# A hybrid decoder layer on one core: where group 0's down projection stands in the first feed-forward, and in which order VectorE takes the mixer's modulation sums

## The chip, the core and the metric

The kernel runs on one core of a Trainium2 chip. The metric is the device time of one execution in microseconds; the time given for a kernel is the median of its runs. The engines are TensorE (PE, with its weight loads PEld), VectorE (DVE), ScalarE (ACT), GpSimd (POOL) and SyncE (SP), whose queue issues all of the transfers spoken of here. In the profile every instruction recorded through the small wrapper class of this kernel has the line L107, so instructions are told apart by their tiles.

## What is computed

One layer of a decoder over 1024 tokens of width 1024, in float32, with a feed-forward (hidden width 2816) ahead of a mixer and another behind it:

```python
(sh1, sc1, g1, sh2, sc2, g2, sh3, sc3, g3) = jnp.split(c_act @ w_mod[l] + b_mod[l], N_MOD, axis=-1)

h = modulate(rms_norm(x, ffn1_norm[l]), sh1, sc1)
x = x + 0.5 * g1[:, None, :] * swiglu(h, ffn1_w_gate[l], ffn1_w_up[l], ffn1_w_down[l])

h = modulate(rms_norm(x, mix_norm[l]), sh2, sc2)
b_gate, c_gate, v, u = jnp.split(h @ w_in[l], [D_CONV, 2 * D_CONV, 3 * D_CONV], axis=-1)
y_conv = short_conv_mixer(b_gate, c_gate, v, conv_w[l])
y_ssm = s5_mixer(u, ...)
y_mix = jnp.concatenate([rms_norm(y_conv, ...), rms_norm(y_ssm, ...)], axis=-1)
x = x + g2[:, None, :] * (y_mix @ w_out[l])

h = modulate(rms_norm(x, ffn2_norm[l]), sh3, sc3)
x = x + 0.5 * g3[:, None, :] * swiglu(h, ffn2_w_gate[l], ffn2_w_up[l], ffn2_w_down[l])
return rms_norm(x, final_norm)
```

`swiglu(h, wg, wu, wd)` is `(silu(h @ wg) * (h @ wu)) @ wd`.

## The kernel before

**Products.** Each float32 operand is split into a high and a low part, and a product takes three matmuls (`mm3`: high by high, high by low, low by high) of 128 x 128 by 128 x 512. The tokens are two halves of 512 (`h` = 0, 1). The hidden width is 11 groups (`NGRP`) of 256, the model width 8 blocks of 128 (`d` or `k`). A group's first part is its gate and up projection, its second part its down projection.

**The first feed-forward.** Groups 0 to 3 are projected plainly, groups 4 to 10 by `seven`, a scheme of Strassen's kind with seven products in place of eight; their activations ("lefts") go to DRAM tiles `kept[g]` (`keep`, an SP transfer for each). The second part of groups 1 to 4 and of 5 to 8 follows, by seven products again, in two calls of `down7` ("fad0", "fad1"). Each call makes two passes p = 0, 1 over seven products; a product takes four lefts of 512 KB each and one granule of weights. Passes p = 0 and 1 write the blocks d = 0, 1, 4, 5 and 2, 3, 6, 7. The lefts of chunk 0 are fetched during group 10's up side, those of chunk 1 during p = 1 of fad0 (`fetch_chunk`, through the argument `then`). Groups 0, 9 and 10 (`LAST[0]`) remain: `last_parts` does them together, for four blocks d and one token half at a time (d outside, h inside), 2 x 2 x 3 x 8 calls of `mm3`, and adds the sum to x by one `scalar_tensor_tensor` for each (d, h). Their activations are fetched by `fetch_last` in p = 1 of fad1, at the products A11, A12 and A22. `after1` squares and sums the new x for the mixer's norm; with the last block of a half it starts that half's norm, whose results `h2` (16 tiles) the mixer's first projection `u` reads. `u` takes four weight tiles at once.

**Weights.** `Weights` holds the weights' order: `stream` lists the raw arrays (1 MB each; two raw buffers) and granules (pairs of pieces). `pump` takes a free slot (three in `ringp`, a fourth in `ring1b` for the mixer), copies the high part on ACT and computes the low part on VectorE; sums of pieces for the seven-product schemes are made on POOL. A raw buffer is loaded again when all of its pieces are split. In the first feed-forward the last arrays are `wl1`, three raw arrays for groups 0, 9 and 10.

**x.** x is not held during the projections. `open_x` gives it space when group 10 starts; `load_x` fetches its eight 512 KB tiles, four then and four at the product A12 of p = 0 of fad0.

**Space.** The pool "A" of `mov` has 20 tiles of 512 KB, the pool "B" (`movB1`) 12. They hold the modulated input and its combinations, the lefts, the tiles that `keep` stores, the modulation weights of the first side work, and `h2`.

**Side work.** A `Clock` counts calls of `mm3`; every `period` ticks it steps a generator. `side2` does modulation sums: `mod_fetch` loads a 512 KB tile `wm` over SP, `mod_tile` multiplies and sums it on VectorE (1.14 to 1.23 us), 24 sums for three vectors, with two tiles in flight. It runs once from fad1 on (period 8) for the vectors of the mixer, and once in the mixer for those of the second feed-forward: added with period 8 ahead of the last `gate_b` calls, stopped by period 1000 ahead of `glu`, and stepped again with period 3 from `w_out((2, 3), 1, 0)` on; a loop behind `w_out((4, 5, 6, 7), 0, 1)` steps what is left, ahead of the norm `n3` of the second feed-forward's input `h3`.

**Order.** The compiler's scheduler orders each engine's instructions by its own simulated times: an instruction whose operands are there in the simulation goes ahead of an earlier one that still waits. Only where `InOrder.strict` is set (the prologue) does the wrapper tie each instruction to the one before it on its engine. An engine runs its queue in the order so fixed.

Of the kernel before, what the change touches and what calls it, by code (L numbers as in the profile page):

```python
# [17 lines left out]
ALU = mybir.AluOpType  # L18
# [3 lines left out]
P = 128  # L22
# [6 lines left out]
NGRP = NF // 2  # L29
# [6 lines left out]

CHUNKS = 2

LAST = ((0, NGRP - 2, NGRP - 1), (NGRP - 2, NGRP - 1))
J = S // TAU  # L40
NB = 8
GB = G // NB
# [16 lines left out]
class Clock:  # L59
# [2 lines left out]

    def __init__(self, period):
        self.now, self.period, self.n, self.since = 0, period, 0, 0
        self.due, self.side = [], deque()

    def after(self, ticks, fn):
        self.n += 1
# [10 lines left out]

    def step(self):  # L80
        if self.side:
            try:
                next(self.side[0])
            except StopIteration:
                self.side.popleft()

    def until(self, done):
        while not done():
# [8 lines left out]
class InOrder:  # L97


    strict = False  # L100

    def __init__(self, tc, engine):
        self.tc, self.engine, self.last = tc, engine, None

    def __getattr__(self, name):
        def call(*args, **kw):
            r = getattr(self.engine, name)(*args, **kw)  # L107
            if self.last is not None and InOrder.strict:
                info = mybir.DependencyInfo(mybir.DependencyClass.NoSync, mybir.DependencyReason.DATA)
                self.tc.add_manual_dep(r.ins, self.last.ins.name, info, reason="order of issue")  # L110
            self.last = r
            return r

        return call
# [114 lines left out]


@with_exitstack
def hymba_layer(ctx: ExitStack, tc, x_d, wm1_d, wmod_d, gu1_d, gs1_d, ds1_d, wl1_d, win_d, wout_d, glu_d, gu2_d, gs2_d, wd2_d, ds2_d, wl2_d, cols_d, cond_d, lam_d, bc_d, out_d):
    nc = tc.nc
    V, A, T, SP = (InOrder(tc, e) for e in (nc.vector, nc.scalar, nc.tensor, nc.sync))

# [51 lines left out]
    def stream(gu, gs, wd, ds, wl, m):  # L287


        for g in range(m):  # L290
            plain([gu[2 * g], gu[2 * g + 1]])
        for g in range(m, NGRP):
            j = len(srcs)
            inner = g == 1
            srcs.extend([gs[g - m, 0], wd, gs[g - m, 1]] if inner else [gs[g - m, 0], gs[g - m, 1]])
            seven = [(i, c) for i in (j, j + 1 + inner) for c in Weights.SEVEN]
            seven = [seven[i : i + 2] for i in range(0, 14, 2)]
            if inner:
                granules.extend(seven[:1] + [[(j + 1, 2 * q), (j + 1, 2 * q + 1)] for q in range(2)] + seven[1:])
            else:  # L300
                granules.extend(seven)
        for c in range(CHUNKS):
            for p in range(2):
                j = len(srcs)
                srcs.extend([ds[c, p, 0], ds[c, p, 1]])
                granules.extend([(j, s), (j + 1, s)] for s in Weights.SECOND)
        plain([wl[i] for i in range(wl.shape[0])])

    stream(gu1_d, gs1_d, None, ds1_d, wl1_d, SEVEN_FROM[0])
    plain([win_d[i] for i in range(8)] + [glu_d] + [wout_d[i] for i in range(4)])  # L310
    stream(gu2_d, gs2_d, wd2_d, ds2_d, wl2_d, SEVEN_FROM[1])
    ws = Weights((V, A, SP, nc.gpsimd), srcs, granules, 2)
# [517 lines left out]
    def kept_for(g, all_seven=True):  # L830

        names = [left for left, _ in SEVEN] if all_seven else ["A11", "A12", "A21", "A22"]
        return {left: scratch.tile([P, 2, HALF], F32, name=f"kept{g}{left}") for left in names}

    kept = {g: kept_for(g, g not in LAST[0]) for g in range(NGRP)}
    afs = {}
    for fi in range(2):
        for i in (2 * fi, 2 * fi + 1):
# [331 lines left out]
                gu_keep(fi, h, pg[h], proj(wu, act[h], f"{name}u{fi}_{h}"), afs, kept, name)  # L1170
            ws.free()

    movs["B"] = es1.enter_context(tc.tile_pool(name="movB1", bufs=12))
    sums_open, first_open = sums_opened()
    clock.side.append(side1())
    clock.period = 4
# [1 line left out]
        gate_up(act1, f"fa{g}", kept[g], g == SEVEN_FROM[0] - 1)  # L1178
    clock.period = 7.75
    lefts = [{left: [] for left, _ in SEVEN} for _ in range(CHUNKS)]  # L1180
    a_last = [{} for _ in LAST[0]]
    HOMES = dict(A11="A", S2="B", A12="A", S3="B", S1="B", A22="A", S4="A")

    def fetch_chunk(c, left, name="fa"):
        for g in range(1 + 4 * c, 5 + 4 * c):
            lefts[c][left].append(fetch(kept[g], left, HOMES[left], f"{name}{g}l"))

    def fetch_last(left):

        if left in ("A11", "A12", "A22"):  # L1190
            i = ("A11", "A12", "A22").index(left)
            for h in range(2):
                for fi in range(2):
                    a_last[i][fi, h] = fetch(kept[LAST[0][i]], f"A{h + 1}{fi + 1}", "A", f"fa{LAST[0][i]}l")

    for g in range(SEVEN_FROM[0], NGRP):
        if g == NGRP - 1:
            while clock.side:
                clock.step()
            side_open.close()  # L1200
            first_open.close()
            open_x(ctx)
            load_x(range(2), (0, 2))
        if g == NGRP - 2:
            pools.pop("first")
        seven(f"fa{g}", lambda: None, kept=kept[g], then=(lambda left: fetch_chunk(0, left)) if g == NGRP - 1 else None)
    down7("fad0", lefts[0], 0, lambda left: fetch_chunk(1, left), lambda left: load_x(range(2), (1, 3)) if left == "A12" else None)
    clock.period = 8
    clock.side.append(side2(mod_mov, (SC2, SH2, G2)))
    down7("fad1", lefts[1], 0, fetch_last)  # L1210
    ws.sums_pool = None
    sums_open.close()
    ring1_open = ExitStack()

    def last_parts():
        for dh in range(2):
            wd = ws.take(3)
            for h in range(2):
                outs = [ps(f"fald{4 * dh + i}_{h}") for i in range(4)]
                for q, (w, a) in enumerate(zip(wd, a_last)):  # L1220
                    for fi in range(2):
                        for i, o in enumerate(outs):
                            mm3(o[:], w, 4 * fi + i, a[fi, h], q == fi == 0, q == 2 and fi == 1)
                    if h:
                        ws.free()
                for i, o in enumerate(outs):
                    d = 4 * dh + i
                    V.scalar_tensor_tensor(out=x[d][h], in0=o[:], scalar=gate[:, 0, d : d + 1], in1=x[d][h], op0=ALU.mult, op1=ALU.add)
                    after1(d, h)

    last_parts()
    while clock.side:
        clock.step()
    es1.close()
    ring1 = ring1_open.enter_context(tc.tile_pool(name="ring1b", bufs=1, side="right"))
    ws.open(ring1, 1)
    ws.pump()


    es2 = ExitStack()  # L1240
# [170 lines left out]
    pools["cact"] = wmp.tile([P, 1024], F32, name="cact2")  # L1411
    SP.dma_start(pools["cact"][:], cact_d[:])
    clock.period = 8
    clock.side.append(side2(lambda name: wmp.tile([P, 1024], F32, tag="wm", name=name, bufs=2)[:], (SC3, SH3, G3)))
    for i in range(4):
        across(i, lambda d, t: SP.dma_start(t, d), y_d, yb[i])
# [66 lines left out]
    while clock.side:  # L1483
        clock.step()
    clock.period = 4
    mods_open.close()
    es2.close()
    movs["B"] = ctx.enter_context(tc.tile_pool(name="movB", bufs=12))
# [35 lines left out]

    clock.side.extend([combos(act3, "h3", "BAA"), combos_last(act3, "h3", "A")])
    a_prev = group0()
    kept = {g: kept_for(g, g not in LAST[1]) for g in range(1, NGRP - 1)}
    HOMES = dict(A11="B", S2="A", A12="B", S3="A", S1="B", A22="A", S4="A")
    lefts = [{left: [] for left in HOMES} for _ in range(CHUNKS)]
    a_last = {}  # L1530
# [67 lines left out]
def _arrays(i):  # L1598
# [5 lines left out]
    for n in (1, 2):  # L1604
        g, u = _tiles(i[f"ffn{n}_w_gate"][0]), _tiles(i[f"ffn{n}_w_up"][0])
        wd = i[f"ffn{n}_w_down"][0]
        m = SEVEN_FROM[n - 1]

        b = wd.reshape(NGRP, 2, P, 2, 512)
        if n == 2:  # L1610
            a["wd2"] = b[0].transpose(1, 2, 0, 3).reshape(P, 2, 1024)
        b = b[list(LAST[n - 1])].transpose(3, 0, 2, 1, 4).reshape(-1, 2, P, 1024)
        a[f"wl{n}"] = b.transpose(0, 2, 1, 3)

        b = wd.reshape(NGRP, 2, P, 2, 2, 2, P)[1 : 1 + 4 * CHUNKS].reshape(CHUNKS, 2, 2, 2, P, 2, 2, 2, P)
# [24 lines left out]
    return {k: np.ascontiguousarray(v) for k, v in a.items()}  # L1640


_ORDER = ["x", "wm1", "wmod", "gu1", "gs1", "ds1", "wl1", "win", "wout", "glu", "gu2", "gs2", "wd2", "ds2", "wl2", "cols", "cond", "lam", "bc"]


# [15 lines left out]
```

## Time and profile before

| | us |
|---|---|
| median of 3 runs | 1750.19 |
| lowest, highest | 1748.85, 1751.76 |
| the profiled execution | 1752.1 |
| its span, first to last instruction | 1750.3 |
| PE busy in the span | 1677.9 |
| DVE busy | 1300.6 |
| ACT busy | 566.0 |
| POOL busy | 351.1 |

The mean granted clock of TensorE is 0.989 of full. The profile has a page with busy times, groups and the chain of waits, and views of single stretches: a table of stretches (busy time of each engine with the number of instructions, the granted clock, the share of time in which the 16 DMA engines were busy, GB/s), the instructions of one engine in order of time (start, length, engine, line, operation, output and inputs, count, and in brackets the idle time before and what ended it), the waits in total, and the transfers with their time from issue to landing. The stretches of the first feed-forward in the profile are group 10's first part from 467 to 505, fad0 from 505 to 590, fad1 from 590 to 668, and the last parts from 668 to 736.

### The profile page before, as it was taken

Reading aid. Unit: us, or ns where it says so; the run is one execution under the profiler, and the core shown is the slowest. Engines: PE = TensorE matmul, PEld = TensorE weight load, DVE = VectorE, ACT = ScalarE, POOL = GpSimd, SP = SyncE. Lnnn points to the kernel's source line nnn. Section 1 sums busy time; section 2 is a strip of 40 time slices with the busy share of each in tenths; the row PEclk is TensorE's granted clock in tenths of the full one; section 3 lists DMA queues with packets and bytes.
Section 4 is the critical chain, followed back from the end, with each engine's and each line's share of the span. In section 5 each row is a group of like instructions: output and inputs, shape, how many; then the busy total and the mean of one; then the engine's idle time right before and its main releaser. Section 6 shows DMA issues by size and latency. Waiting matters only on the chain.

```text
span 1750.3 us, 20808 instructions
## 1 busy us (share of the span) xinstructions
PE 1677.9 (96%) x7532; PEld 1379.6 (79%) x7532; DVE 1300.6 (74%) x2286; ACT 566.0 (32%) x934; POOL 351.1 (20%) x241
## 2 busy tenths in 40 slices
PE   4999999999999999999999899989999999999996
PEld 3788887878787888887877778778888888888886
DVE  7999999999855687744656977967777666676656
ACT  4223234444322221332113424423343443322221
POOL 0000132222222221100000022023323322333211
PEclk9999999999999999999999999999999999999998
DMA  8245544444597877134654450113444334669312
GB/s 319 85 145 196 207 167 165 182 169 178 196 391 266 326 256 292 56 84 149 210 157 140 144 191 25 48 46 135 157 162 173 147 133 156 239 242 366 115 49 96
DMA packets 101080, 304.54 MB, mean 174 GB/s; under 512 B 19057, under 2 KB 34673, under 8 KB 89842
## 3 DMA queue, kind: packets, MB, share of 16 engines
q1 hardware_dynamic: 100978, 303.22, 48.4%
q8 instruction: 59, 0.97, 0.2%
q14 instruction: 43, 0.35, 0.1%
HBM read 212.47 MB, written 86.51 MB: 171 GB/s over the span
## 4 chain that ended last, share of the span: by engine, by line
PE 76%; DVE 14%; DMA 5%; issue 2%; POOL 1%; ACT 1%; SPq 1%; DVEq 0%; POOLq 0%; ACTq 0%
PE wo L107 4%; PE fald L107 3%; DVE w L107 3%; PE p L107 2%; PE fb10d L107 2%; PE fbd_0B L107 2%; PE fbd_1B L107 2%; PE u L107 2%; DMA swz<-si 2%; PE b L107 1%; DVE x L107 1%; PE c L107 1%; PE fa3u L107 1%; PE fb0g L107 1%; PE fa2g L107 1%
## 5 line engine op out<-in xcount | busy, mean ns | idle before, releaser
L107 ACT CAST w<-raw 128x512 fp32r<-128x512 f32 (+1 forms) x358 | 236.2, 689 | 484.3 <-issue 75.0
L107 DVE TENSOR_TENSOR w<-raw,w 128x512 fp32r<-128x512 f32 (+1 forms) x358 | 295.9, 845 | 107.3 <-ACT w L107 106.5
L164 POOL TENSOR_TENSOR sums<-raw 128x512 f32<-128x512 f32 x50 | 71.4, 1429 | 451.5 <-DMA raw<-in_gs 263.3
L173 POOL TENSOR_TENSOR raw<-sums,raw 128x512 f32<-128x512 f32 x50 | 77.7, 1554 | 371.1 <-DVE w L107 358.9
L175 POOL TENSOR_TENSOR raw<-raw 128x512 f32<-128x512 f32 x50 | 77.5, 1549 | 89.6 <-DVE w L107 73.0
L107 DVE CUSTOM_DVE_ANT_0 wm<-wm,cact 128x1024 f32<-128x1024 f32 x56 | 76.6, 1375 | 16.9 <-DMA wm<-in_wmod 16.9
L165 POOL TENSOR_TENSOR raw<-raw 128x512 f32<-128x512 f32 x50 | 77.3, 1547 | 3.2
L366 POOL TENSOR_TENSOR n3aq<-n3aq,n3aq 128x512 f32<-128x512 f32 x5 | 8.3, 1666 | 281.4 <-DMA wm<-in_wmod 255.7
L107 PE MATMUL p<-h,w 128*128 128x512 f32 x192 | 50.0, 423 | 8.0 <-DVE h L107 5.1
L107 DVE TENSOR_TENSOR w<-sums,w 128x512 fp32r<-128x512 f32 x50 | 52.5, 1063 | 3.6 <-ACT w L107 3.0
L107 PEld LDWEIGHTS p<-h,w 128*128 128x128 f32 x192 | 39.4, 207 | 18.4 <-DVE h L107 6.4
L107 PE MATMUL v<-h,w 128*128 128x512 f32 x192 | 46.9, 395 | 0.0
L107 PE MATMUL c<-h,w 128*128 128x512 f32 x192 | 46.6, 395 | 0.0
L107 PE MATMUL wo<-oa,w 128*128 128x512 f32 x192 | 45.6, 392 | 0.9 <-DVE w L107 0.7
L107 PE MATMUL b<-h,w 128*128 128x512 f32 x192 | 45.6, 394 | 0.0
L107 PE MATMUL wo<-ob,w 128*128 128x512 f32 x192 | 45.5, 392 | 0.0
L107 PE MATMUL u<-h,w 128*128 128x512 f32 x192 | 44.7, 392 | 0.2 <-DVE h L107 0.2
L107 PEld LDWEIGHTS wo<-oa,w 128*128 128x128 f32 x192 | 35.8, 188 | 9.0 <-DVE w L107 1.1
L107 PEld LDWEIGHTS u<-h,w 128*128 128x128 f32 x192 | 35.7, 188 | 8.2 <-DVE h L107 0.6
L107 PEld LDWEIGHTS wo<-ob,w 128*128 128x128 f32 x192 | 35.8, 188 | 7.7 <-DVE ob L107 0.4
L107 PEld LDWEIGHTS b<-h,w 128*128 128x128 f32 x192 | 35.6, 188 | 7.1
L107 PEld LDWEIGHTS c<-h,w 128*128 128x128 f32 x192 | 35.4, 188 | 7.0
(1565 smaller groups left out, 4056.2 us busy)
## 6 DMA issues: line engine op xcount, KB each, us to landing
raw<-in_gs SPq DMA_DIRECT2D x34, 1024.0 KB, 5.5
wm<-in_wmod SPq DMA_DIRECT2D x56, 512.0 KB, 5.3
raw<-in_ds SPq DMA_DIRECT2D x16, 1024.0 KB, 7.2
raw<-in_gu SPq DMA_DIRECT2D x10, 1024.0 KB, 7.0
mw<-in_wm SPq DMA_DIRECT2D x8, 1024.0 KB, 12.8
x<-in_x SPq DMA_DIRECT2D x16, 512.0 KB, 8.0
raw<-in_win SPq DMA_DIRECT2D x8, 1024.0 KB, 5.4
raw<-in_wl SPq DMA_DIRECT2D x5, 1024.0 KB, 6.7
```

What stands on the lines that cost most here:

```text
L107: r = getattr(self.engine, name)(*args, **kw)
L164: self.G.tensor_tensor(out=f, in0=r[2], in1=r[1], op=ALU.subtract)
L165: self.G.tensor_tensor(out=r[1], in0=r[1], in1=r[0], op=ALU.subtract)
L173: self.G.tensor_tensor(out=r, in0=s["t3"], in1=r, op=ALU.add)
L175: self.G.tensor_tensor(out=r, in0=self.chunk(j, 3), in1=r, op=ALU.subtract)
L366: nc.gpsimd.tensor_tensor(out=a, in0=a, in1=sq[:, :n], op=ALU.add)
```

## The change

Four things are changed. Group 0's second part is done by itself, by `down2`, directly behind group 10's first part and ahead of fad0; its weights are a raw array of their own (`wd1`) behind group 10's, its activations are fetched where chunk 0's A11 lefts were, and these are fetched behind `down2` in the program. x is loaded whole when group 10 starts. The last parts are groups 9 and 10 alone, by `down`, with the token half outside and the blocks inside; the pool `movB1` is closed and the fourth slot `ring1b` opened ahead of them, and the four weight tiles are taken at once and given back at the end; the period there is 7. And in the mixer's side work each VectorE instruction of a step is tied to the VectorE instruction issued before it in the program (`pinned`).

```diff
-LAST = ((0, NGRP - 2, NGRP - 1), (NGRP - 2, NGRP - 1))
+LAST = (NGRP - 2, NGRP - 1)
...
     def step(self):
         if self.side:
+            if self.pin is not None:
+                self.pin.pinned = True
             try:
                 next(self.side[0])
             except StopIteration:
                 self.side.popleft()
+            if self.pin is not None:
+                self.pin.pinned = False
...
-            if self.last is not None and InOrder.strict:
+            if self.last is not None and (InOrder.strict or self.pinned):
...
+        if m > 1:
+            plain([wd])
...
-    stream(gu1_d, gs1_d, None, ds1_d, wl1_d, SEVEN_FROM[0])
+    stream(gu1_d, gs1_d, wd1_d, ds1_d, wl1_d, SEVEN_FROM[0])
...
-    movs["B"] = es1.enter_context(tc.tile_pool(name="movB1", bufs=12))
+    movB1_open = ExitStack()
+    movs["B"] = movB1_open.enter_context(tc.tile_pool(name="movB1", bufs=12))
...
+    def fetch_all(tiles, g):
+        for h in range(2):
+            for fi in range(2):
+                tiles[fi, h] = fetch(kept[g], f"A{h + 1}{fi + 1}", "A", f"fa{g}l")
+
+    def fetch_now(left):
+
+        if left == "A11":
+            fetch_all(a_first, 0)
+        else:
+            fetch_chunk(0, left)
+
     def fetch_last(left):
 
-        if left in ("A11", "A12", "A22"):
...
+        if left in ("A11", "A12"):
+            i = ("A11", "A12").index(left)
+            fetch_all(a_last[i], LAST[i])
...
-            load_x(range(2), (0, 2))
+            load_x(range(2))
...
-        seven(f"fa{g}", lambda: None, kept=kept[g], then=(lambda left: fetch_chunk(0, left)) if g == NGRP - 1 else None)
-    down7("fad0", lefts[0], 0, lambda left: fetch_chunk(1, left), lambda left: load_x(range(2), (1, 3)) if left == "A12" else None)
-    clock.period = 8
+        seven(f"fa{g}", lambda: None, kept=kept[g], then=fetch_now if g == NGRP - 1 else None)
+    down2(a_first, 0, "fa0", (0, 1))
+    fetch_chunk(0, "A11")
+    down7("fad0", lefts[0], 0, lambda left: fetch_chunk(1, left))
+    clock.period = 7
     clock.side.append(side2(mod_mov, (SC2, SH2, G2)))
     down7("fad1", lefts[1], 0, fetch_last)
     ws.sums_pool = None
     sums_open.close()
+    movB1_open.close()
     ring1_open = ExitStack()
-
-    def last_parts():
...
-    last_parts()
+    ring1 = ring1_open.enter_context(tc.tile_pool(name="ring1b", bufs=1, side="right"))
+    ws.open(ring1, 1)
+    ws.pump()
+    w = ws.take(4)
+    for h in range(2):
+        down(h, [w[0], w[2], w[1], w[3]], a_last, 0, "fal", after1)
+    ws.free(4)
     while clock.side:
         clock.step()
     es1.close()
-    ring1 = ring1_open.enter_context(tc.tile_pool(name="ring1b", bufs=1, side="right"))
-    ws.open(ring1, 1)
-    ws.pump()
...
     clock.period = 8
+    clock.pin = V
     clock.side.append(side2(lambda name: wmp.tile([P, 1024], F32, tag="wm", name=name, bufs=2)[:], (SC3, SH3, G3)))
...
     clock.period = 4
+    clock.pin = None
...
-        if n == 2:
-            a["wd2"] = b[0].transpose(1, 2, 0, 3).reshape(P, 2, 1024)
-        b = b[list(LAST[n - 1])].transpose(3, 0, 2, 1, 4).reshape(-1, 2, P, 1024)
+        a[f"wd{n}"] = b[0].transpose(1, 2, 0, 3).reshape(P, 2, 1024)
+        b = b[list(LAST)].transpose(3, 0, 2, 1, 4).reshape(-1, 2, P, 1024)
```

`down2` is the helper that the second feed-forward already uses for its group 0: for four blocks d and a token half at a time it computes each output in a PSUM bank of its own (two calls of `mm3`) and adds it to x at once; a weight tile is given back after its four blocks.

More of the change, by code (lines that the diff above doesn't have):

```diff
@@ L64, in __init__ @@
         self.now, self.period, self.n, self.since = 0, period, 0, 0
-        self.due, self.side = [], deque()
+        self.due, self.side, self.pin = [], deque(), None
     def after(self, ticks, fn):
@@ L102, in __init__ @@
     def __init__(self, tc, engine):
-        self.tc, self.engine, self.last = tc, engine, None
+        self.tc, self.engine, self.last, self.pinned = tc, engine, None, False
     def __getattr__(self, name):
@@ L231, in hymba_layer @@
 @with_exitstack
-def hymba_layer(ctx: ExitStack, tc, x_d, wm1_d, wmod_d, gu1_d, gs1_d, ds1_d, wl1_d, win_d, wout_d, glu_d, gu2_d, gs2_d, wd2_d, ds2_d, wl2_d, cols_d, cond_d, lam_d, bc_d, out_d):
+def hymba_layer(ctx: ExitStack, tc, x_d, wm1_d, wmod_d, gu1_d, gs1_d, wd1_d, ds1_d, wl1_d, win_d, wout_d, glu_d, gu2_d, gs2_d, wd2_d, ds2_d, wl2_d, cols_d, cond_d, lam_d, bc_d, out_d):
     nc = tc.nc
@@ L293, in stream @@
             j = len(srcs)
-            inner = g == 1
+            inner = g == m == 1
             srcs.extend([gs[g - m, 0], wd, gs[g - m, 1]] if inner else [gs[g - m, 0], gs[g - m, 1]])
@@ L833, in kept_for @@
         return {left: scratch.tile([P, 2, HALF], F32, name=f"kept{g}{left}") for left in names}
-    kept = {g: kept_for(g, g not in LAST[0]) for g in range(NGRP)}
+    kept = {g: kept_for(g, 0 < g < NGRP - 2) for g in range(NGRP)}
     afs = {}
@@ L1180, in hymba_layer @@
     lefts = [{left: [] for left, _ in SEVEN} for _ in range(CHUNKS)]
-    a_last = [{} for _ in LAST[0]]
+    a_first, a_last = {}, [{} for _ in LAST]
     HOMES = dict(A11="A", S2="B", A12="A", S3="B", S1="B", A22="A", S4="A")
@@ L1186, in fetch_chunk @@
             lefts[c][left].append(fetch(kept[g], left, HOMES[left], f"{name}{g}l"))
-    def fetch_last(left):
-        if left in ("A11", "A12", "A22"):
[L1191 to L1194, printed above, removed]
+    def fetch_all(tiles, g):
[7 more added lines that the diff above has]
+            fetch_chunk(0, left)
+    def fetch_last(left):
+        if left in ("A11", "A12"):
+            i = ("A11", "A12").index(left)
+            fetch_all(a_last[i], LAST[i])
     for g in range(SEVEN_FROM[0], NGRP):
@@ L1212, in hymba_layer @@
     sums_open.close()
+    movB1_open.close()
     ring1_open = ExitStack()
-    def last_parts():
[L1216 to L1229, printed above, removed]
-    last_parts()
+    ring1 = ring1_open.enter_context(tc.tile_pool(name="ring1b", bufs=1, side="right"))
[5 more added lines that the diff above has]
+    ws.free(4)
     while clock.side:
@@ L1526, in hymba_layer @@
     a_prev = group0()
-    kept = {g: kept_for(g, g not in LAST[1]) for g in range(1, NGRP - 1)}
+    kept = {g: kept_for(g, g not in LAST) for g in range(1, NGRP - 1)}
     HOMES = dict(A11="B", S2="A", A12="B", S3="A", S1="B", A22="A", S4="A")
@@ L1640, in _arrays @@
     return {k: np.ascontiguousarray(v) for k, v in a.items()}
-_ORDER = ["x", "wm1", "wmod", "gu1", "gs1", "ds1", "wl1", "win", "wout", "glu", "gu2", "gs2", "wd2", "ds2", "wl2", "cols", "cond", "lam", "bc"]
+_ORDER = ["x", "wm1", "wmod", "gu1", "gs1", "wd1", "ds1", "wl1", "win", "wout", "glu", "gu2", "gs2", "wd2", "ds2", "wl2", "cols", "cond", "lam", "bc"]
 def kernel(**inputs):
```

## The prediction

> **What bounds the kernel now.** I read the page's head first, then a table of stretches, then the order of instructions on TensorE (PE) in the stretches that lose time.
>
> ```profile
> span 1750.3 us, 20808 instructions
> PE 1677.9 (96%) x7532; PEld 1379.6 (79%) x7532; DVE 1300.6 (74%) x2286; ACT 566.0 (32%) x934; POOL 351.1 (20%) x241
> ```
>
> PE is the bound, and no matmul is added or removed. So the change can only win or lose in the 72 us in which PE stands, and in the lower granted clock around such a stand. The table of stretches (start:end, length, busy PE, PEld, DVE, ACT, POOL, granted clock, DMA share, GB/s) shows where that is near the change:
>
> ```profile
> 505.00:527.00 22.00, 22.00 (x99) 18.24 (x98) 13.87 (x20) 6.16 (x11) 2.16 (x2) 1.00 1.00 368
> 543.40:562.60 19.20, 15.34 (x49) 11.13 (x49) 10.79 (x11) 5.09 (x10) 11.38 (x8) 0.82 0.51 190
> 724.00:755.00 31.00, 29.79 (x140) 23.84 (x141) 24.04 (x53) 10.51 (x16) 2.59 (x2) 1.00 0.19 69
> 975.00:986.00 11.00, 7.09 (x31) 5.84 (x32) 9.61 (x26) 4.01 (x6) 0.00 (x0) 0.90 0.42 138
> 1029.00:1036.00 7.00, 6.12 (x26) 4.45 (x25) 7.00 (x7) 3.03 (x4) 5.77 (x3) 1.00 0.49 142
> 1143.00:1156.00 13.00, 10.42 (x37) 7.54 (x36) 12.46 (x20) 1.24 (x2) 3.40 (x1) 0.87 0.00 1
> ```
>
> The largest loss that the first part of the change can reach is 543.4 to 562.6, in the first chunk's second projection (`down7` "fad0"), at the turn from p = 0 to p = 1. PE's own rows there, with the idle time and its releaser in brackets, and a row of the chain of waits for twelve undisturbed matmuls:
>
> ```profile
> 543.74 0.74 PE L107 MATMUL fad_0A<-fa1lA,w 128*128 128x512 f32 x2 [0.31 <-ACT w L107]
> 546.66 0.57 PE L107 MATMUL fad_0A<-fa1lA,w 128*128 128x512 f32 x1 [1.71 <-DVE w L107]
> 556.58 1.52 PE L107 MATMUL fad_0B<-fa3lS,w 128*128 128x512 f32 x3 [1.81 <-ACT w L107]
> 562.78 2.72 PE fad_0A L107 x12
> ```
>
> Two lefts with two outputs each are computed there, 4 x 12 matmuls: 4 x 2.72 = 10.9 us. They take 19.2, so 8.3 us are lost: 0.31 + 1.71 + 1.81 = 3.8 idle and 4.5 at the lower clock (0.82 in the table). The wait is for split weights, and behind them for the raw weights:
>
> ```profile
> 543.07 0.62 ACT L107 CAST w<-raw 128x512 fp32r<-128x512 f32 x1 [14.26 <-DMA raw<-in_ds]
> 527.80 1.30 DVE L107 TENSOR_TENSOR w<-raw,w 128x512 fp32r<-128x512 f32 x2 [0.48 <-ACT w L107]
> 529.73 0.32 SPq L107 DMA_DIRECT2D kept10A<-fa10A  x1
> 530.15 0.37 SPq L107 DMA_DIRECT2D fa1lS<-kept1S  x1
> 532.98 1.28 SPq L107 DMA_DIRECT2D raw<-in_ds  x2
> 480.00:500.00 20.00, 20.00 (x90) 16.55 (x89) 7.70 (x12) 6.30 (x12) 6.29 (x5) 1.00 1.02 407
> 500.00:520.00 20.00, 20.00 (x90) 16.59 (x89) 16.50 (x22) 7.42 (x13) 6.37 (x5) 1.00 1.00 376
> 520.00:540.00 20.00, 20.00 (x90) 16.59 (x89) 10.92 (x16) 2.81 (x5) 0.00 (x0) 1.00 0.87 322
> ```
>
> The buffers of p = 0 are free about 528, but the load goes out at 533, in SP's order behind group 10's last store (held to 529.7, until its tile was computed), four lefts and an x tile. It then lands at 543, ten us later, in a stretch whose DMA engines are full. What fills them is the fetching of a whole chunk of lefts (28 tiles of 512 KB) just as the first product begins.
>
> **The change part by part.** *Group 0 moved ahead.* Its 16 outputs x 2 x 3 = 96 matmuls go from the last parts to 505 to 527: 8 x 2.72 = 21.8 us of PE, moved, not added; net 0. The 16 outputs of groups 9 and 10 keep their 16 additions into x, so `down2` adds 16 on VectorE:
>
> ```profile
> L107 DVE SCALAR_TENSOR_TENSOR x<-fald,gate,x x16: 746/751/751, 683.2 to 744.8; 128x512 f32<-128x512 f32 x16
> PE fb0d L107 <- DVE x L107: 5.1, 4, 2.0
> ```
>
> That is 16 x 0.75 = 12.0 us. One output takes PE 6 matmuls, 1.36 us, so VectorE keeps pace, with six PSUM banks (8.2 us) between. It was busy 13.9 of 22 us in this stretch, of which the adds of fad0 (505 to 527) move on. The last parts lose four fetches and one of three raw loads to the stages ahead of fad0; nothing waits for these there now. I cost this at 0; where the cover is gone, the same helper in the second feed-forward gives the price: PE waited 5.1 us there, VectorE being full (12.46 of 13 us).
>
> What it brings is time: fad0 starts 21.8 us later, and the fetches of its lefts do not. At the turn to p = 1, now about 565, the first chunk's lefts and all of x have landed, the stores of group 10 are long out, and the raw load finds an emptier DMA. The later turns show what it then needs:
>
> ```profile
> raw<-in_ds SPq DMA_DIRECT2D x16, 1024.0 KB, 7.2
> 614.85 0.93 SPq L107 DMA_DIRECT2D raw<-in_ds  x2
> 631.13 0.50 PE L107 MATMUL fad_0A<-fa7lA,w 128*128 128x512 f32 x1 [1.14 <-DVE w L107]
> ```
>
> Five us from the queue and three from the landing (10 to 7.2) are more than the 3.8 us of idle. I take the whole 8.3 us back; the bounds are 0 and -8.3. The second chunk's turn (1.14 us idle, held by weights again) stays as it is: its modulation sums are stepped every 7 ticks instead of 8, 176 ticks / 7 = 25 steps against 208 / 8 = 26, as dense per stage; 0, bounds -1.1 and +1.1.
>
> A rule speaks for a smaller prize. The Trainium skill, TensorE: Matmul & The Clock Gate, Part 1 (The HAM clock gate), has the clock fall only after an idle window of about 3.4 us. No gap here is that long, so by the rule only the 3.8 idle us could be won, and the sum below would be -2.9 instead of -7.4. The row shows 0.82 in just this stretch and 1.00 before it, so the measurement decides against it, and it gets no chance of its own.
>
> *What the move costs.* Group 10 now fetches group 0's four tiles where it fetched chunk 0's A11; these are issued about 480 to 487, as the A11 tiles are now, in time for 505. A11 of chunk 0 is fetched last in the program and is needed first, at 527. From 478 SP has to issue x 2 MB, raw wd and ds 3, stores 2, group 0 2, six lefts 12, A11 2: 23 MB. At 0.40 MB/us (407 and 376 GB/s in the table) that ends at 478 + 57 = 535, 8 us late. If SP again holds S4's lefts to 530 and A11 goes behind them, it lands 532 + 9 = 541, 14 late (9 is between the issue-to-landing times below). In the better case A11 takes the buffers of group 10's stores from about 512 and nothing is late. The scheduler also has PE take another left first when one is late, as rows of PE here show; one left covers 5.4 us.
>
> ```profile
> 479.87 0.59 SPq L107 DMA_DIRECT2D fa1lA<-kept1A  x1
> 487.39 0.43 SPq L107 DMA_DIRECT2D x<-in_x  x1
> fa1lA<-kept1A SPq DMA_DIRECT2D x2, 512.0 KB, 7.6
> fa4lA<-kept4A SPq DMA_DIRECT2D x2, 512.0 KB, 9.2
> 518.79 0.39 PE L107 MATMUL fad_1B<-fa1lS,w 128*128 128x512 f32 x1
> 519.02 0.84 PE L107 MATMUL fad_0A<-fa1lA,w 128*128 128x512 f32 x3
> ```
>
> Bounds 0 and +14; 8 late less 5.4 covered is 2.6, and I take +3. All of x before group 10 costs nothing: seven of its eight transfers are out with that of 487.39 already.
>
> *Last parts and the mixer's start.* Now all of the first token half comes before the second, so its norm and its `h2` (8 x 2 x 0.67 = 11 us of VectorE) lie under the second half's 21.8 us of PE, not behind its end. At 724 to 755 PE loses 31.00 - 29.79 = 1.2 us, while VectorE works off h2 ahead of the last four additions. I take -1.1; bounds -1.2 and +2.3. The loss would be the fourth u weight, whose slot is free only with the last matmul: 1.06 on ACT and 1.23 on VectorE (rows below); three other weights cover it. Opening the fourth slot earlier otherwise changes nothing on PE.
>
> *The pinned sums.* Grouped by stretch, the sums (`wm`) run as follows, and the chain of waits has, in the third stall of the gated norm:
>
> ```profile
> 955.00:968.00 13.00, 4.88 (x4) 0.94 0.54 176
> 968.00:1013.00 45.00, 12.07 (x9) 0.96 0.41 131
> 1013.00:1050.00 37.00, 15.49 (x11) 1.00 0.60 206
> 977.12 1.06 ACT w L107
> 978.20 1.23 DVE w L107
> 979.50 1.14 DVE wm L107
> 981.89 1.14 DVE wm L107
> 983.72 1.92 PE nBabc L107 x8
> 1064.81 1.41 DVE L107 SCALAR_TENSOR_TENSOR h3t<-x,scl,n3abc 128x512 f32<-128x512 f32 x2
> ```
>
> The program steps four sums in `gate_b` and the other 20 only from `w_out((2, 3), 1, 0)` on, about 1013; the compiler's reordering has drawn nine ahead. Pinned, these leave 968 to 1013. In the chain two of them stand ahead of nBabc; the weight split ahead of them waits for ACT in any case. So 2 x 1.14 less the pauses between small steps, -2.0; at best the whole stand of 11.0 - 7.09 = 3.9. They reappear behind 1013: eleven took up to 37 us, a little over 3 each, as each fetch waits for one of two buffers; so 20 from 1016 may last to 1076, past the start of `h3` (1064.81). Scale and shift are complete with the twelfth, about 1052; up to four gate sums (4 x 1.23 = 4.9 us) may mix with h3 ahead of group 0 of the second feed-forward, and one may hold a weight split, as in 1029 to 1036 (0.9 idle). I take +1.0, bounds 0 and +4.9. Net -1.0.
>
> **Sum.** -8.3 + 3.0 - 1.1 - 1.0 = -7.4 us. The profiled execution took 1752.1 us (span 1750.3 and 1.8 around it), so 1744.7; it lies 1.9 above the median of the runs, 1750.2, against which I state 1742.8.
>
> **The rivals.** About 0.2% (3.5 us) is what the measurement can tell from no change: below 1746.7 is faster, above 1753.7 slower. *A11 late, slower.* SP sends A11 behind S4, 14 us late; with half of one left's cover PE stands 14 - 2.7 = 11.3 us and pays the 4.5 of the lower clock: 15.8 in place of 8.3, +7.5 - 2.1 = +5.4, 1755.6. It decides once idle and clock together exceed 8.3 + 2.1 = 10.4 us. For it: 23 MB do not fit into 49 us, and SP held S4 to 530. Against: PE is reordered, buffers come free from 512. Chance 0.24. *The stand moves, no change.* `down2` waits for VectorE as in the second feed-forward (5.1 us), or A11 is 5 us worse than I take: -7.4 + 5.1 = -2.3, 1747.9. For it: that row; against: VectorE has only 13.9 of 22 us to do. Chance 0.16. *Sums too late:* +4.9 instead of +1.0, 1746.7 or just under; chance 0.07. *The pin does nothing,* because simulated readiness already gives this order: 1743.8; the nine early sums speak against it; 0.05.
>
> **How the numbers follow.** My forecast has 0.48; with the last two rivals faster is 0.60, same 0.16, slower 0.24. The likeliest case alone runs from 1739 (no late A11) to 1746. The range reaches up to the slower rival and a little over it, 1757, and down to 1737, where the nBabc stand goes whole.
>
> **What would show it.** Right: no idle of PE at the turn to p = 1 of fad0 and clock 1.00 there; fb0d-like waits absent from `down2`; no `wm` from 968 to 1013; nBabc about 2 us earlier after its statistics. Wrong: idle ahead of the first fad_0A with a lefts transfer as releaser; `down2` waiting for x; sums behind h3t; the second feed-forward's stalls other than now, which I leave unchanged.

## The result, and the profile after

| | before | after |
|---|---|---|
| device time, median (lowest to highest) | 1749.52 us (1745.65 to 1751.76, 4 runs) | 1772.54 us (1770.84 to 1773.98, 4 runs) |
| the profiled execution, its span | 1752.1 us, 1750.3 us | 1770.84 us, 1768.7 us |

The changed kernel is slower: ratio 1.0134, 95% interval 1.0113 to 1.0154, some 23 us by the medians. The two profiled executions are 18.4 us apart in span; the one of before is a long run of its kernel and the one after a short run, so the sums below, which go by spans, come out 4.6 us smaller than the medians.

The head of the page after, as that of before:

```profile
span 1768.7 us, 20825 instructions
PE 1678.8 (95%) x7532; PEld 1380.2 (78%) x7532; DVE 1310.7 (74%) x2302; ACT 565.7 (32%) x934; POOL 347.8 (20%) x241
```

PE has the same 7532 matmuls and the same busy time within 1 us. What has grown is the time in which it stands: 1768.7 - 1678.8 = 89.9 us, where it was 72.4. The view of waits says for what. These are its rows at the places that the change touches (engine, tile, releaser: us in total, times, longest):

```profile
PE fad_0A L112 <- DMA fa1lA<-kept1A: 18.5, 1, 18.5
PE n3ast L112 <- DVE n3aq L112: 4.2, 1, 4.2
PE n3bbc L112 <- DVE n3brb L112: 2.3, 1, 2.3
PE fb0u L112 <- DVE w L112: 0.8, 1, 0.8
PE u L112 <- DVE w L112: 0.8, 1, 0.8
PE nBabc L112 <- DVE nBarb L112: 0.7, 1, 0.7
```

One wait of 18.5 us, for the first A11 left of chunk 0, is new, and so are three waits of 7.3 us together at the third norm and the start of the second feed-forward (`n3`, `fb0`). The table of stretches shows the first part of it (start:end, length, busy PE, PEld, DVE, ACT, POOL, granted clock, DMA share, GB/s): group 0's second part, the stand behind it, the turn to p = 1, and the start of the mixer.

```profile
504.00:526.80 22.80, 22.79 (x101) 18.55 (x99) 15.66 (x23) 3.01 (x5) 7.94 (x6) 1.00 0.85 335
526.80:545.20 18.40, 0.00 (x0) 0.00 (x0) 3.13 (x5) 1.66 (x3) 0.11 (x1) 0.56 0.93 346
580.00:602.00 22.00, 22.00 (x99) 18.22 (x98) 14.94 (x19) 5.71 (x11) 8.22 (x6) 1.00 0.54 192
736.00:767.00 31.00, 30.20 (x143) 24.27 (x142) 26.67 (x47) 14.65 (x22) 8.34 (x5) 1.00 0.20 69
```

`down2` runs without a gap (22.79 of 22.80), and the turn to p = 1 is full at clock 1.00, where before it had 15.34 of 19.20 at 0.82. Between them PE does nothing for 18.4 us. The two orders that explain it are those of SyncE's queue and of ScalarE. SyncE after, around the stand (start, time, what it issues):

```profile
513.91 0.32 SPq L112 DMA_DIRECT2D fa1lA<-kept1A  x1
527.49 0.32 SPq L112 DMA_DIRECT2D kept10A<-fa10A  x1
...
532.62 0.61 SPq L112 DMA_DIRECT2D fa4lS<-kept4S  x1
533.58 0.40 SPq L112 DMA_DIRECT2D fa1lA<-kept1A  x1
...
538.95 0.32 SPq L112 DMA_DIRECT2D fa4lA<-kept4A  x1
```

Group 0's tiles are out long before, by 487. The row of 513.91 is the first left of A22. Behind it in the queue stands a store of group 10, which goes out at 527.49; then come three more of A22, another store, the four of S4, and only then, from 533.58, A11. The first lands in time for a matmul at 545.27. ScalarE shows why the store was not ready:

```profile
516.00 0.62 ACT L112 CAST w<-raw 128x512 fp32r<-128x512 f32 x1 [10.27 <-PE fa0d L112]
518.99 0.62 ACT L112 CAST w<-raw 128x512 fp32r<-128x512 f32 x1 [2.37 <-DMA raw<-in_ds]
524.20 0.62 ACT L112 CAST w<-raw 128x512 fp32r<-128x512 f32 x1 [4.58 <-POOL raw L178]
524.73 0.61 ACT L112 CAST fa10A<-fa10uu 128x512 fp32r<-128x512 f32 x1
```

The first half of the kept tile (`fa10A`) is cast at 524.73, although VectorE had its source done at 504.1 (its row there starts at 503.41 and is 0.69 long). In ScalarE's order it stands behind three casts of down weights, which wait in turn for `down2` to give a weight buffer back, for a transfer and for GpSimd.

The pinned sums (`wm`) after, by stretch (length, busy DVE with the count, clock, DMA share, GB/s):

```profile
965.00:978.00 13.00, 3.91 (x4) 0.84 0.52 162
978.00:1022.00 44.00, 0.97 (x1) 1.00 0.15 48
1022.00:1050.00 28.00, 13.33 (x9) 1.00 0.65 217
1050.00:1083.00 33.00, 13.70 (x11) 0.90 0.52 167
```

They keep the program's order: four in `gate_b`, 20 from 1022 to 1083. All engines in the last of these stretches, in the columns of the table above:

```profile
1050.00:1083.00 33.00, 28.81 (x125) 23.85 (x124) 22.43 (x45) 4.69 (x7) 4.82 (x3) 0.90 0.52 167
```

PE is idle for 4.2 of the 33 us, ahead of `n3ast`, the sums of the third norm. Behind that wait it works at a lower clock: from `n3ast` to `n3abc` the same 29 matmuls take 8.0 us (1070.25 to 1078.25), and before they took 5.7 (1058.00 to 1063.72), so 2.3 more are lost. The rows of `n3ast` after and before:

```profile
1070.25 1.87 PE L112 MATMUL n3ast<-one,n3aq 128*128 128x1 f32 x8 [4.19 <-DVE n3aq L112]
```

```profile
1058.00 0.95 PE L107 MATMUL n3ast<-one,n3aq 128*128 128x1 f32 x8
```

Before, PE was busy throughout at this place:

```profile
1043.00:1083.00 40.00, 40.00 (x190) 33.50 (x190) 28.29 (x54) 14.46 (x20) 6.63 (x4) 1.00 0.11 32
```

### The profile page after: what moved, and what is told of

Same layout as the page of the kernel before. It is cut to its first block, busy times and chain, and to the rows that moved or that the text cites. A ratio compares the mean times of both kernels' runs of the same rounds, so it can differ in the third digit from the quotient of the medians.

```text
span 1768.7 us, 20825 instructions
## 1 busy us (share of the span) xinstructions
PE 1678.8 (95%) x7532; PEld 1380.2 (78%) x7532; DVE 1310.7 (74%) x2302; ACT 565.7 (32%) x934; POOL 347.8 (20%) x241
## 4 chain that ended last, share of the span: by engine, by line
PE 46%; DVE 7%; DMA 3%; issue 1%; ACT 0%; SPq 0%; POOL 0%; DVEq 0%; ACTq 0%
PE fb10d L112 2%; PE u L112 2%; PE b L112 2%; PE wo L112 2%; PE fbd_0B L112 2%; PE fbd_1B L112 2%; PE v L112 2%; DVE x L112 1%; PE fbd_1C L112 1%; PE fbd_0C L112 1%; PE fbd_1A L112 1%; PE fbd_0A L112 1%; DMA wm<-in_wmod 1%; PE c L112 1%; PE gl L112 1%; DVE w L112 1%
## 5 line engine op out<-in xcount | busy, mean ns | idle before, releaser
L112 DVE CUSTOM_DVE_ANT_0 wm<-wm,cact 128x1024 f32<-128x1024 f32 x56 | 72.1, 1290 | 25.0 <-DMA wm<-in_wmod 25.0
```

## The experiments

Theory: the change loses at two places that have nothing to do with each other. A11 of chunk 0, wanted first, is fetched last, behind a held store; and the pinned sums come late in the mixer, at the pace of their transfers, ahead of the third norm. The rivals are stated with each run. Medians are compared with the kernel before on the same chip: 1750.21 us for the first four, 1748.94 for the next four, 1747.84 for the last. Between batches the ratios are compared.

### The two parts apart

Without the pin, `e1`:

```diff
-    clock.pin = V
```

> The changed kernel without the pin on VectorE; group 0 stays ahead of fad0. In the changed kernel the start of glu lay 9.7 us behind that of before and the end 18.4 us behind. Theory: the 8.7 us between the two come from the pin alone (sums moved behind 1013, into the norm and the input of the second feed-forward): 1772.5 - 8.7 = about 1764, the span about 1760, the stand of 18.5 us ahead of fad0 unchanged. Rival: they come from another instruction order that the move itself brings to the mixer: 1772, with the stands at n3ast and in wo as in the changed kernel.

Measured: 1764.69 us, ratio 1.0086 (1.0064 to 1.0108).

The A11 lefts of chunk 0 fetched early, directly behind group 0's tiles, with the pin (`e2`) and without it (`e3`):

```diff
     def fetch_now(left):
         if left == "A11":
             fetch_all(a_first, 0)
-        else:
-            fetch_chunk(0, left)
+        fetch_chunk(0, left)
...
     down2(a_first, 0, "fa0", (0, 1))
-    fetch_chunk(0, "A11")
```

> The changed kernel with the A11 lefts of chunk 0 fetched during group 10, right behind group 0's four tiles, instead of behind down2; the pin stays. Theory: A11 was late because it stood last in SP's queue, behind a store that was held and behind 8 other lefts; then fad0 starts at 527 without a stand, the 12.6 us lost at this place go and the 8.3 us of the turn to p = 1 stay won: 1772.5 - 12.6 - 8.3 = about 1752. Rival: the transfers of this stretch do not fit into it, whatever their order: another left or the weights come late, PE stands 8 us or more between 527 and 570, and the time stays above 1760.

> Both: A11 fetched early and no pin. Theory (the two losses are independent): 1772.5 - 12.6 - 8.3 - 8.7 = about 1743, 0.4% faster than before. Rival (the move has no gain of its own to show): within 0.2% of before, 1746 to 1753.

Measured: 1752.51 us, ratio 1.0009 (0.9998 to 1.0021), with the pin; 1743.53 us, ratio 0.9965 (0.9951 to 0.9979), without. The pin alone on the kernel before (`e4`, with the few lines of `Clock.step` and `InOrder` that carry it):

> The kernel before with the pin alone. Theory: the sums move from 968 to 1013 to behind 1013 here too and cost 8.7 us net: 1749.5 + 8.7 = about 1758, with a stand of about 4 us at n3ast and none above 1 us at nBabc. Rival: the pin costs only in the order that the move brings; then 1747 to 1750, by the stand at nBabc (3.9 us before) that it takes away.

Measured: 1758.78 us, ratio 1.0046 (1.0032 to 1.006). All four came out close to what the theory gave. The waits of `e1`, and then those of `e4`:

```profile
PE fad_0A L112 <- DMA fa1lA<-kept1A: 17.5, 1, 17.5
PE nBabc L112 <- DVE nBarb L112: 3.9, 1, 3.9
```

```profile
PE n3ast L111 <- DVE n3aq L111: 4.6, 1, 4.6
PE n3bbc L111 <- DVE n3brb L111: 2.3, 1, 2.3
```

Without the pin the stand for A11 is there and the `n3` waits are not; with the pin alone it is the other way round. So the two do not share a cause, and they add: the pin costs 8.4 us (after against `e1`, 0.48% by the ratios), 9.0 (`e2` less `e3`) and 8.6 (`e4` less before), wherever it is taken away or added. The order of the fetches costs 1.25%, 21.9 us (after against `e2`). And in `e2` PE goes from `down2` to the first product without a gap:

```profile
503.98 21.92 PE L112 MATMUL fa0d<-fa0lA,w 128*128 128x512 f32 x96
525.74 0.84 PE L112 MATMUL fad_0A<-fa1lA,w 128*128 128x512 f32 x3
```

SyncE of `e2` is held by the same stores, and longer than in the changed kernel:

```profile
490.79 0.38 SPq L112 DMA_DIRECT2D fa1lA<-kept1A  x1
...
517.25 0.32 SPq L112 DMA_DIRECT2D fa4lA<-kept4A  x1
532.97 0.32 SPq L112 DMA_DIRECT2D kept10A<-fa10A  x1
...
543.10 0.42 SPq L112 DMA_DIRECT2D fa4lS<-kept4S  x1
```

The hold is not removed but costs nothing: what is now late is S4, issued up to 543.1, and PE wants that last. `e3` beats both kernels, by 6.7 us the one before on its chip: the move of group 0 pays with A11 fetched in time and without the pin. (`e8` below gets as much without the move, 0.9972 against 0.9965; the intervals overlap.)

### What holds A11 back

`e5` takes the stores of group 10 out of SyncE's queue (on top of `e1`):

```diff
-            SP.dma_start(kept[left][:], t[:].bitcast(F32))
+            (A if name == "fa10" else SP).dma_start(kept[left][:], t[:].bitcast(F32))
```

> The changed kernel without the pin, as in e1 (1764.7 us), with the A11 lefts of chunk 0 still fetched last in the program; only the stores of group 10's kept tiles are issued on ScalarE's queue instead of SyncE's. Theory: A11 is late because SyncE stands 12.3 us behind a store whose tile is not yet computed, and everything behind it moves by that. Then SyncE issues A11 some 10 us earlier, the 17.5 us stand ahead of the first fad_0A shrinks to 3 to 8 us, and the time is 1747 to 1755 us. Rival: the transfers themselves, or the buffers that A11 goes into, hold it. Then SyncE stands at another instruction, the stand stays at 12 us or more, and the time is 1760 us or more.

Measured: 1759.05 us, ratio 1.0066 (1.0051 to 1.0081), between the two expectations and nearer to the rival's. The stand is 13.1 us, above the rival's bound, and SyncE stands at another instruction, as the rival said. Its rows, and its longest wait there:

```profile
523.92 0.32 SPq L112 DMA_DIRECT2D fa2lS<-kept2S  x1
532.65 0.32 SPq L112 DMA_DIRECT2D fa3lS<-kept3S  x1
...
533.70 0.38 SPq L112 DMA_DIRECT2D fa1lA<-kept1A  x1
```

```profile
SPq L112 <- DMA kept10A<-fa10A: 8.3, 1, 8.3
```

SyncE no longer issues the store, yet it waits for its landing. The built program shows why: each transfer, whichever queue issues it, waits for one of eight counters of landings, which are taken in turn, so a transfer cannot go out before the one with the same counter has landed. The third left of S4 and the late store of group 10 share one:

```
ScalarE  kept10A21 <- fa10A21   landing counter 3
SyncE    fa3lS4    <- kept3S4   landing counter 3, the next to take it
```

So the theory's place (the queue) was too narrow and the rival's "buffers or volume" was not yet tested. `e9` tells these apart. It leaves the queue as it is and issues the last two stores behind A11 in the program, out of the way in both senses (on top of `e1`):

```diff
-            SP.dma_start(kept[left][:], t[:].bitcast(F32))
+            store = lambda: SP.dma_start(kept[left][:], t[:].bitcast(F32))
+            later_stores.append(store) if name == "fa10" and left in ("A21", "A12") else store()
...
     fetch_chunk(0, "A11")
+    while later_stores:
+        later_stores.pop(0)()
```

> The kernel of e1 (changed kernel without the pin, 1764.7 us, stand of 17.5 us) with the last two stores of group 10's kept tiles issued on SyncE behind the A11 lefts of chunk 0 instead of ahead of them; nothing else moves, and A11 is still the last fetch of the chunk. Theory: the two stores, whose tiles are split only at 525 to 529, are what holds A11 back, in whichever queue they are, as each transfer also waits for the landing of the eighth before it in program order. Then SyncE goes on to A11 at 523 to 527, the stand ahead of the first fad_0A is 5 to 9 us, and the time is 1749 to 1756 us. Rival: the volume of the transfers, or group 0's tiles, whose buffers A11 takes, hold it as well. Then the stand stays above 12 us and the time is 1758 us or more.

Measured: 1755.81 us, ratio 1.0045 (1.0028 to 1.0062). SyncE runs through, and the stand is halved, to 8.9 us:

```profile
524.49 0.32 SPq L112 DMA_DIRECT2D fa1lA<-kept1A  x1
...
528.33 0.32 SPq L112 DMA_DIRECT2D fa4lA<-kept4A  x1
```

```profile
534.60 1.62 PE L112 MATMUL fad_0A<-fa1lA,w 128*128 128x512 f32 x3 [8.91 <-DMA fa1lA<-kept1A]
```

```profile
520.00:540.00 20.00, 11.09 (x44) 8.69 (x43) 7.92 (x11) 2.85 (x6) 3.59 (x3) 0.83 1.03 419
```

The theory holds for 8.6 of the 17.5 us, on the edge of its range (5 to 9 us of stand expected). The two stores are also 1 MB that no longer goes ahead of A11, 2.5 us at the pace below, so a part of the 8.6 may be volume too. The other 8.9 us are read as volume; no run takes it away. The DMA engines are full (share 1.03, 419 GB/s) and the lefts go out 1.2 to 1.3 us apart, 0.52 MB each. That share is the rival's, by volume and not by buffers: SyncE waits only 1.3 us in all for `fa0d`, whose matmuls give A11's buffers back. With the fetches in the order of use, as in `e2`, both shares vanish, since neither the volume nor the hold then lies ahead of A11.

### What makes the pinned sums dear

`e6` keeps the pin and the sums of `e2`, and takes the transfers away: 22 of the 24 sums read the first two loaded tiles again. It leaves out the loading of the other modulation weights of the second feed-forward, so it does not compute the layer.

```diff
-    def mod_fetch(home):
+    def mod_fetch(home, again=None):
...
-            r = home(f"wm{n}_{b}_{i}")
-            SP.dma_start(r, wmod_d[n - 2, b, :, i, :])
+            r = again
+            if again is None or n not in (SH3, SC3, G3):
+                r = home(f"wm{n}_{b}_{i}")
+                SP.dma_start(r, wmod_d[n - 2, b, :, i, :])
...
-        mod_fetch(home)
+        mod_fetch(home, r)
```

> The kernel of e2 (A11 fetched early, sums pinned, 1752.5 us), in which 22 of the 24 pinned sums read the first two loaded tiles again: the loading of the other modulation weights for scale, shift and gate of the second feed-forward is left out. The instructions of VectorE and their order stay. Theory: the pinned tail is slow because each sum waits for a transfer into one of two buffers, which it can't get before the sum two places ahead is done. Then the stands of n3ast, n3bbc and the start of the second feed-forward go, and the time is 1743 to 1746 us. Rival: the sums cost by their own time on VectorE and by where the program has them. Then those stands stay and the time is 1749 us or more.

Measured: 1740.33 us, ratio 0.9949 (0.9929 to 0.9969), below the theory's range. Sums of `e6`, in the columns of the sums above:

```profile
1010.00:1040.00 30.00, 21.46 (x16) 1.00 0.10 36
1040.00:1070.00 30.00, 1.22 (x1) 1.00 0.00 1
```

With no transfer to wait for, 16 sums go by in 30 us and one is left after 1040, and none of the waits at `n3` remains. VectorE's order did not stay as the expectation has it: in `e2` as built seven sums stand among or behind the last additions into x ahead of `n3`, in `e6` one. In the changed kernel VectorE waits 14.8 us for these transfers from 1013 to 1085:

```profile
DVE wm L112 <- DMA wm<-in_wmod: 14.8, 7, 3.9
```

So the cost is not the 24 x 1.2 us of VectorE; it is the transfers. Sums wait for one into one of two buffers (seven waits there), the pin makes that wait VectorE's whenever a sum is next in the order, and the last sums come to stand beside the norm. `e6` takes away the waits and this place together, and does not tell them apart. Against `e3` the ratio is 0.16% lower, 2.8 us: the pin's gain at `nBabc` without its price. The intervals overlap, so that size is not secured by the times alone; the waits at `nBabc` (none in `e6`, 3.9 in `e3`) say the same.

`e7` keeps the transfers and the pin, and moves the sums' place in the program (on top of `e2`, ahead of `glu`, where stepping is all but switched off):

```diff
-    clock.period = 1000
+    clock.period = 8
```

> The kernel of e2 with the pin, in which the 20 sums left behind the gated norm are stepped from its start on, every 8 ticks (the clock's period of 1000 at that place becomes 8). Theory: the pin costs because the program's place for these sums is late, not because they are in the program's order. Then the sums are spread over 945 to 1060, the stand of n3ast goes, and the time is 1742 to 1747 us. Rival: any order that is fixed costs, as VectorE then waits for a transfer with other work ready behind it. Then sums stand in the gated norm with idle VectorE ahead of them, and the time stays at 1750 us or more.

Measured: 1745.22 us, ratio 0.9986 (0.9977 to 0.9995), within the theory's range, 0.23% below `e2`. Its waits and its sums:

```profile
PE nBabc L112 <- DVE nBarb L112: 4.4, 1, 4.4
```

```profile
930.00:985.00 55.00, 9.74 (x8) 0.94 0.43 137
985.00:1010.00 25.00, 7.18 (x5) 1.00 0.44 145
```

Thirteen sums now stand ahead of 1010, where `e2` has eight and `e3` sixteen. The wait at `nBabc` is back with them (4.4), and the waits at `n3` are gone. That is close to what the compiler's own order did (`e3`, 0.9965): most of the cost lay in the place that the pin fixes. How much of it stays with a better place is open. By the medians half is left, 0.21% against `e3`, which would be the rival's part. By the traces nothing is left: from the first `u` of the mixer to the end it takes 1024.2 us in `e2`, 1014.2 in `e3` and 1013.6 in `e7`. The profiled `e7` loses its time ahead of `u`, which it reaches 5.2 us later than `e2`, on another chip; up to the gated norm the programs of the three are the same.

### The turn by itself

`e8` is the kernel before with the store edit of `e5`; it moves group 0 nowhere.

> The kernel before (1750.2 us) with the stores of group 10's kept tiles issued on ScalarE's queue instead of SyncE's. It measures the term of 8.3 us by itself. Theory: five us of that raw load's lateness come from SyncE's queue, held by the last store, and the rest from the landing. Then the raw load goes out at about 528.5 instead of 533, the turn of fad0 to p = 1 loses 0 to 4 us instead of 8.3, and the time is 1742 to 1747 us. Rival: the landing alone holds it, in full DMA engines. Then the turn still loses 7 us or more and the time is 1749 to 1751 us.

Measured: 1744.14 us, ratio 0.9972 (0.9962 to 0.9982). The raw load goes out at 529.84 (533 before), and the stretch that had 15.34 of 19.20 at 0.82 is full:

```profile
529.84 0.93 SPq L107 DMA_DIRECT2D raw<-in_ds  x2
```

```profile
543.40:562.60 19.20, 19.20 (x84) 15.43 (x83) 14.09 (x18) 6.81 (x13) 7.64 (x5) 1.00 0.73 259
```

The whole stall is gone with 3 us on the queue and 2 from the landing: ScalarE's first copy of these weights starts at 538.02, and at 543.07 before. The first matmul of chunk 1 starts at 583.00, and at 589.82 before: 6.8 us earlier, with 1.1 us lost anew at an earlier left, A12 (517.24). So the theory holds, at the better end of its range of 0 to 4 us for what is left: without the held store there is no stall, and moving group 0 was not needed to be rid of it.

## Why the prediction was wrong

It had 1742.8 us and no more than 1757; the time is 1772.5. PE's starts from the four traces, in us, give each term by itself:

| PE starts | before | after | `e2` | `e3` |
|---|---|---|---|---|
| first `fad_0A` | 505.19 | 545.27 | 525.74 | 525.77 |
| first matmul of chunk 1 (`fad_0A<-fa5lA`) | 589.82 | 623.45 | 601.90 | 601.93 |
| first `u` of the mixer | 735.88 | 748.22 | 726.73 | 726.31 |
| first `c` of the mixer | 783.50 | 795.30 | 773.79 | 773.37 |
| first `gl` of the mixer | 946.03 | 955.73 | 934.83 | 933.51 |

**The turn, -8.3: right.** From the first `fad_0A` to chunk 1 it takes 84.6 us before and 76.2 in `e2` and `e3`: 8.5 won. Idle alone was 3.8, so more than the idle was to be won, as taken. Not all of the 4.5 beside it is the clock: 0.82 over 19.2 us is 0.18 x 19.2 = 3.5, and 1.0 has no row. A rule that would have left only the idle time does not fit this.

**`down2` at 0: right.** It has no wait. What it adds to x lies beside PE, as the 22.79 of 22.80 us show.

**A11 late, +3.0, bounds 0 to +14: this is the step that failed.** Measured, it is 18.5 idle and 78.2 - 76.2 = 2.0 at the lower clock, +20.5. Three things in it were wrong. First, the prediction named two delays, 8 us by volume and the hold of the store, and took them as alternatives. They add: `e9` shows 8.9 for the volume, and the hold another 8.6. Second, the landing was put at 541, from an issue at 532 and 9 us; it was issued at 533.58 and landed about 545, as the other lefts had a full queue ahead of it. Third, 5.4 us were taken off because PE would do another left first; with the text's own 14 and nothing taken off, its sum would have been -8.3 + 14 - 1.1 - 1.0 = +3.6. PE did no other left first: in the changed program as built the 24 matmuls of A11 stand first, and PE waits in that order. The rows of before in which PE took another left first were the scheduler's choice ahead of the run: the built program of before has them in that order. They are no dodge made when a transfer is late.

The rival "A11 late, slower" was the right mechanism with the right releaser, at 0.24, and priced at +5.4 for the same reasons: it still had half a left's cover, and the lateness of 14 where 18.5 came.

**Last parts and the mixer's start, -1.1: wrong by little.** From chunk 1 to `u` it takes 146.06 us before, 21.76 of which belong to the moved group 0: 124.3. It takes 124.8 after and 124.4 in `e3`. The stand that the text meant lies behind the first `u`, so the measure has to reach `c`, which follows: 171.9 us before without group 0, 171.9 after, 171.4 in `e3`. At most 0.5 was won. The old waits there (1.0 for `n2bst`, 0.2 for `h`) are gone in the changed kernel, but 0.8 for the split `u` weight, which the text named as the loss, and 0.4 for `n2ast` are new.

**The pin, -1.0, bounds 0 to +4.9 for its tail: the sign was wrong.** The gain was there and larger than taken: -3.2 at `nBabc` (3.9 to 0.7) against -2.0. The tail was seen too, 20 sums that may last to 1076 (1083 in fact, in a program that is 9.7 us later by the start of `gl`), but priced at the wrong place. The prediction counted four gate sums mixing with h3, +1.0. What they delay first stands before h3: the additions of `wo`'s outputs into x, and through them the squares of the third norm. In these rows of VectorE after, three additions come only behind a sum that waited for its transfer, and the norm's squares (`n3aq`) behind them, through GpSimd; the last add of squares is at 1069.50, and PE's `n3ast` starts at 1070.25, 4.19 us late:

```profile
1059.99 1.23 DVE L112 CUSTOM_DVE_ANT_0 wm<-wm,cact 128x1024 f32<-128x1024 f32 x1 [1.01 <-DMA wm<-in_wmod]
...
1061.14 2.07 DVE L112 SCALAR_TENSOR_TENSOR x<-wo,gate,x 128x512 f32<-128x512 f32 x3
...
1066.25 0.69 DVE L112 TENSOR_TENSOR n3aq<-n3aq,n3aq 128x512 f32<-128x512 f32 x1 [1.17 <-POOL n3aq L373]
```

At `n3ast` 4.2 us are lost and 2.3 at the lower clock behind it, at `n3bbc` and `fb0u` another 3.1; with -3.2 that makes +6.4, against the 8.4 to 9.0 that the runs give. The other 2 us or so have no row that is the pin's alone: a wait of `wo` for ScalarE grew from 0.2 to 1.4 us, but in `e1`, without the pin, to 2.0. The rival "sums too late" had the mechanism with half its price, as it left out the norm and the clock.

By spans, up to `u`: -0.3 (group 10 ended 0.3 earlier) - 8.5 + 20.5 + 0.5 = +12.2, and `u` starts 12.3 later. Behind `u` the spans differ by another 6.1. From `u` to `gl` the changed kernel is 2.6 us shorter (PE's waits at `yy` are 3.3 us there, 5.2 before), a gain that the prediction had no term for and that `e1` and `e3` have without the pin; from `gl` on it is 8.7 longer. So two terms of five were wrong by more than their own bounds, A11 and the pin's tail.

## What to carry to other kernels

A transfer that is wanted first must be issued first: when a fetch list is rearranged, put every item's need beside its place, and add up the delays ahead of it, volume, a held store, and any counter shared in turn, instead of taking the largest. Let nothing cover a late operand because a trace shows another order: the order of a queue is fixed before the run. And before work is pinned to the place that the program gives it, ask how good that place is; here 20 sums with two buffers stood ahead of a norm that PE waits for, and moving the place gave back half of the loss by the medians, all of it by the traces.

## What the runs showed of the hardware

A stand of 18.5 us cost only 2.0 us more in clock: the granted clock is 0.50 from 545 to 549 and 1.00 from 549.4 on, some 4 us after PE starts again at 545.27, and PE's rows are then as short as before.

```profile
545.27 1.62 PE L112 MATMUL fad_0A<-fa1lA,w 128*128 128x512 f32 x3 [18.48 <-DMA fa1lA<-kept1A]
...
550.21 0.85 PE L112 MATMUL fad_0A<-fa4lA,w 128*128 128x512 f32 x3
```

The Trainium skill, TensorE: Matmul & The Clock Gate, Part 1 (The HAM clock gate), puts the change to full speed around 4 us into sustained work; this trace agrees. By the rule's other half, that the clock falls after an idle window of about 3.4 us, the turn of before, whose gaps were 1.8 us at most, should have kept its clock. It did not: the granted clock is 0.50 from 547.0 to 550.0 and from 557.2 to 560.2, each time behind a gap (1.71 and 1.81 us), and 8.5 us came back where only 3.8 were idle. There the measurement decides.
